# A wide column pair's sums: a tile ring of their own, made in place, at a higher priority

## The chip, the core and the metric

The kernel runs on one core of a Trainium2 chip. The metric is the device time of one execution in microseconds (us). The kernel before was timed in three runs; one further execution was recorded by the hardware profiler, and all rows come from it. Engines are named as in the profile: PE is the matrix engine (PEld its weight loads), DVE the vector engine, ACT the scalar engine, POOL the general engine, SP the engine whose queue issues the DMAs.

## The reference, cut to what matters

A batch of one sequence of 256 tokens, width 2048, goes through four layers, all in 32-bit floating point, and a last norm.

- Layer 1: norm, one input projection, sparse attention (an indexer picks 64 keys for each query) beside a multi-scale pooling branch, output projection, norm, residual; then a channel mixer: up-projection to 8192, a causal convolution over three tokens, gelu(gate) * val, down-projection.
- Layer 2: the same frame with latent attention (two low-rank projections, rotary positions) beside a gated linear recurrence, and again a channel mixer.
- Layers 3 and 4, the hybrid layers: one input projection feeds four branches of four heads each. They are attention with a forget bias (`fox`), differential attention (`diff`: the difference of two softmaxes, a norm over each head), block attention (`moba`) and gated linear attention (`gla`, with a norm over each head). Each branch's output is multiplied by silu of its gate, and an output projection adds to the residual.

The projection that the change touches is a plain matrix product, `h @ w_in` (h is 256 x 2048), whose columns are cut into these parts:

```python
h = rms_norm_2(x, norm_g)
p = split_columns(jnp.einsum("bsd,de->bse", h, w_in))
```

## The kernel before, in words

Activations are kept transposed: 128 features on the partitions, 256 tokens along the free axis. Every 32-bit factor is split into a high and a low part, and a product is high*high + low*high + high*low. Weights arrive as 899 packed tiles of 128 x 1024 (`new_sub`, L136 to L152): a DMA on SP's queue brings one in (L143), ACT copies its high part (L147), DVE subtracts to get the low part (L148). One such tile holds eight units of 128 x 128. Five raw buffers and four of each split part are kept ahead; these instructions have a priority offset of 3000.

`projT` (from L161) multiplies columns of 128 output features over all K blocks. In its wide form (n is 1 or 2 columns and there are more than four K blocks, `hold` and `hooks` unused) each column has a PSUM buffer of its own, 512 wide: the high weights meet both parts of x at once (L177, 512 columns), the low weights meet the high part of x (L178, 256 columns). So a finished column has two halves that must be added. `summed()` does it: ACT copies the second half out of PSUM (L193), DVE adds the first half to it (L194), and `evac` then works on the sum, mostly a multiplication with the norm's factor (`ev_mul`, L433). The PSUM pool `pp` has four buffers, so two wide pairs; the pool `pa`, four more, serves everything else. `projV` (from L209) makes values with the roles of the operands exchanged: over 16 K blocks 96 matmuls of 512 columns (L218 to L220), two `pp` buffers.

The order of the instructions on each engine is not written out. A planner takes the instructions in program order as priorities, works out a timeline beforehand by its own cost model, and gives each engine at each moment the ready instruction with the best priority; a tile's buffer is given out in the same process, and an instruction whose tile has no free buffer is not ready. `tc.high_priority(offset=n)` moves a block ahead by n instructions of program order (a negative n moves it back). The evacuations of projections have the offset `EVAC = 100`, the matmuls of the GLA levels -250, and the end of a layer up to 20000. On the chip each engine then executes its queue strictly in that order.

Work tiles of 128 x 2 x 256 come from the pool `wk`, tag `w2`, ten buffers, among them the two of `summed()`. Tiles of 128 x 8 x 256 come from `actp` (`a8`), 13 buffers.

In a hybrid layer (`hybrid`, from L798 on) the program order is: the first projections and `fox_q`; the GLA value projection; the six levels of GLA (DVE subtractions L936 and L937, ACT exponent L938, DVE products L940 and L941, matmuls L922, masked copies L925), its state and outputs (L956 to L994), and `norm_trans` (ACT squares L886, a square root L260, DVE scaling L891, PE transposes L896, DVE copy L897); the load of the lambda vectors (L1001, into a `w2` tile); the four pairs of `diff_q` and `diff_k` into the `a8` tile `dq`; moves of `dq` for the rotary positions; the `diff_v` projection; `fox_q`, second pair; the differential scores and values (L1036 to L1058) with `norm_trans`; `fox_k`, `fox_v`, `moba_q`, and so on.

Of the kernel before, what the change touches and what calls it, by code (L numbers as in the profile page):

```python
# [10 lines left out]
F32 = mybir.dt.float32  # L11
# [3 lines left out]
AF = mybir.ActivationFunctionType  # L15
OP = mybir.AluOpType

P = 128
T = 256
# [46 lines left out]
def kernel(  # L66
# [17 lines left out]
    ap_ = ctx.enter_context(tc.tile_pool(name="actp", bufs=13))  # L84
    rawp = ctx.enter_context(tc.tile_pool(name="rawp", bufs=5))
    hlp = ctx.enter_context(tc.tile_pool(name="hlp", bufs=4))
    wk = ctx.enter_context(tc.tile_pool(name="wk", bufs=10))
    sm = ctx.enter_context(tc.tile_pool(name="sm", bufs=6))
    pp = ctx.enter_context(tc.tile_pool(name="pp", bufs=4, space=PS))
    pa = ctx.enter_context(tc.tile_pool(name="pa", bufs=4, space=PS))  # L90
# [1 line left out]
    V, S, G, TE = nc.vector, nc.scalar, nc.gpsimd, nc.tensor  # L92

    def a8(dt=F32, shape=None):
        return ap_.tile(shape or [P, 8, T], dt, tag="a8", name="a8")

    def w2(dt=F32, shape=None):
        return wk.tile(shape or [P, 2, T], dt, tag="w2", name="w2")
# [8 lines left out]
    def pc(name, i=0, n=1):  # L107
        o, w = PRM[name]
        return prm_t[:, o + i : o + i + n]
# [42 lines left out]
    def blk(key, units=1):  # L152
        if ws["u"] == 8:
            new_sub()
        u = ws["u"]
        assert u + units <= 8
        plan.append((ws["n"] - 1, u, key))
        ws["u"] = u + units
        return ws["h"][:, u * P : (u + units) * P], ws["l"][:, u * P : (u + units) * P]

    def projT(ks, cols, key, xs, evac, hooks={}, hold=False, wide=None):  # L161


        n = len(cols)
        if wide is None:
            wide = len(ks) > 4 and n <= 2 and not hold and not hooks
        pts = [pp.tile([P, 2, T], F32, tag="pp", name="pp") for _ in range(n if wide else (n + 1) // 2)]
        for i, k in enumerate(ks):
            if i in hooks:
                hooks[i]()  # L170
            x = xs(k)
            first, last = i == 0, i == len(ks) - 1
            cs = []
            for ci, c in enumerate(cols):
                h, l = blk(key(k, c))
                if wide:
                    TE.matmul(pts[ci], h, x, start=first, stop=False, skip_group_check=True)  # L177
                    TE.matmul(pts[ci][:, 0], l, x[:, 0], start=False, stop=last, skip_group_check=True)  # L178
                    continue
                o = pts[ci // 2][:, ci % 2]  # L180
                TE.matmul(o, h, x[:, 0], start=(first and ci % 2 == 0), stop=False, skip_group_check=True)  # L181
                TE.matmul(o, l, x[:, 0], start=False, stop=False, skip_group_check=True)  # L182
                cs.append((o, h))
                if n <= 2:
                    TE.matmul(o, h, x[:, 1], start=False, stop=last, skip_group_check=True)  # L185
            if n > 2:
                for o, h in cs:
                    TE.matmul(o, h, x[:, 1], start=False, stop=last, skip_group_check=True)  # L188

        def summed():  # L190
            rest, u = w2(), w2()
            for j in range(n):
                S.activation(out=rest[:, j], in_=pts[j][:, 1], func=AF.Copy)  # L193
                V.tensor_tensor(out=u[:, j], in0=pts[j][:, 0], in1=rest[:, j], op=OP.add)  # L194
            return u

        def evacs():
            with tc.high_priority(offset=EVAC):
                if wide:
                    evac(0, summed())  # L200
                else:
                    for b in range((n + 1) // 2):
                        evac(b, pts[b])

        if hold:
            return evacs
        evacs()

    def projV(ks, key, xs, evac):  # L209
# [129 lines left out]
    class Post:  # L339
# [4 lines left out]
        def evac(self, c, ps):  # L344
            last, n = c == KT - 1, 1 if c >= KT - 2 else 2
            if c == 0:
                self.m = [a8() for _ in range(2)]
                self.acc = w2()
            with tc.high_priority(offset=20000 if last else 0):
                sq = w2() if c else self.acc  # L350
                S.activation(out=sq[:, 0:n], in_=ps[:, 0:n], func=AF.Square)
                if last:
                    self.sq = sq[:, 0]
                elif c:
                    V.tensor_tensor(out=self.acc[:, 0:n], in0=self.acc[:, 0:n], in1=sq[:, 0:n], op=OP.add)
            for j in range(n):
                V.tensor_scalar(out=self.m[(c + j) // 8][:, (c + j) % 8], in0=ps[:, j],
                                scalar1=pc(self.g, c + j), scalar2=None, op0=OP.mult)
# [994 lines left out]
```

## Time and profile before

| | us |
|---|---|
| median of the three timed runs | 2824.79 |
| lowest and highest of them | 2821.60, 2825.44 |
| profiled execution | 2810.94 |
| its span in the trace | 2809.2 |
| PE busy | 2728.4 |
| PEld busy | 2419.7 |
| DVE busy | 1919.1 |
| ACT busy | 1465.1 |

Busy time is the sum of an engine's instruction times in the span. Matmuls follow each other so closely that a matmul's own duration is longer than the distance to the next one; that distance is what counts for a row of them. PEclk is the share of its full clock that PE was granted in a stretch: 1.00 is 2.4 GHz and 0.50 is 1.2 GHz.

### The profile page before, as it was taken

How to read it: one execution, taken by the hardware profiler on the slowest of the kernel's cores; microseconds unless marked ns; L12 is line 12 of the kernel's file. 1: busy time of each engine (PE TensorE's matmuls, PEld its weight loads, DVE VectorE, ACT ScalarE, POOL GpSimd, SP SyncE). 2: the span in 40 equal slices, each digit the busy share in tenths (PEclk: the TensorE clock that was granted, in tenths of full speed). 3: DMA queues.
4: the chain of work that ended last, by engine and by line, in shares of the span. 5: the costliest groups of instructions: out<-in, count | busy, mean ns of one | idle time of the engine just before them, and what ended most of it. 6: DMA issues, size and time to landing. Idle time of an engine off the chain costs nothing.

```text
span 2809.2 us, 42670 instructions
## 1 busy us (share of the span) xinstructions
PE 2728.4 (97%) x16682; PEld 2419.7 (86%) x16682; DVE 1919.1 (68%) x3125; ACT 1465.1 (52%) x2165; POOL 5.8 (0%) x10
## 2 busy tenths in 40 slices
PE   9999999999999999999999999979899998889998
PEld 8888998888888988998888888968688997778897
DVE  6867588777655887587777655856567667465756
ACT  6455456655544675456555544634445554444554
POOL 0000000000000000000000000000000000000000
PEclk9999999999999999999999999979899998889999
DMA  7545545555555454545555555525355554434553
GB/s 252 172 166 175 190 160 188 189 192 189 189 192 167 167 184 129 188 164 185 185 186 187 188 187 180 188 85 184 114 180 169 186 181 135 139 122 160 170 186 134
DMA packets 133290, 483.45 MB, mean 172 GB/s; under 512 B 15136, under 2 KB 16224, under 8 KB 132576
## 3 DMA queue, kind: packets, MB, share of 16 engines
q1 hardware_dynamic: 133088, 480.73, 51.2%
q8 instruction: 130, 2.13, 0.3%
q14 instruction: 72, 0.59, 0.1%
HBM read 476.73 MB, written 2.10 MB: 170 GB/s over the span
## 4 chain that ended last, share of the span: by engine, by line
PE 61%; DVE 2%; ACT 1%; issue 0%; DVEq 0%; ACTq 0%
PE pp L177 25%; PE pp L178 13%; PE pp L181 4%; PE pp L182 4%; PE pp L188 2%; PE pp L218 2%; PE pp L220 2%; PE pp L219 2%; PE pp L185 1%; PE pa L424 0%; PE pa L1105 0%; PE pa L428 0%; DVE a L925 0%; PE pa L896 0%; ACT L260 0%
## 5 line engine op out<-in xcount | busy, mean ns | idle before, releaser
L177 PE MATMUL pp<-a,h 128*128 128x512 f32 x5056 | 1777.6, 396 | 3.5 <-DVE w L194 3.5
L148 DVE TENSOR_TENSOR l<-raw,h 128x1024 fp32r<-128x1024 f32 (+1 forms) x900 | 1100.6, 1223 | 735.9 <-ACT h L147 691.8
L147 ACT ACTIVATE h<-raw 128x1024 fp32r<-128x1024 f32 (+1 forms) x900 | 953.4, 1059 | 1060.6 <-PE pp L177 608.1
L178 PE MATMUL pp<-a,l 128*128 128x256 f32 x5056 | 1421.4, 281 | 0.0
L177 PEld LDWEIGHTS pp<-a,h 128*128 128x128 f32 x5056 | 949.9, 188 | 223.3 <-DVE w L194 4.1
L178 PEld LDWEIGHTS pp<-a,l 128*128 128x128 f32 x5056 | 957.7, 189 | 2.7 <-issue 1.0
L181 PE MATMUL pp<-a,h 128*128 128x256 f32 x1472 | 392.2, 288 | 15.2 <-ACT a L242 6.9
L182 PE MATMUL pp<-a,l 128*128 128x256 f32 x1472 | 389.8, 286 | 0.0
L181 PEld LDWEIGHTS pp<-a,h 128*128 128x128 f32 x1472 | 287.3, 195 | 17.3 <-ACT a L242 7.8
L182 PEld LDWEIGHTS pp<-a,l 128*128 128x128 f32 x1472 | 287.2, 195 | 0.6 <-DVE l L148 0.4
L185 PE MATMUL pp<-a,h 128*128 128x256 f32 x544 | 153.9, 283 | 0.0
L188 PE MATMUL pp<-a,h 128*128 128x256 f32 x928 | 140.6, 286 | 0.0
L218 PE MATMUL pp<-h,a 128*128 128x512 f32 x328 | 129.9, 396 | 0.0
L220 PE MATMUL pp<-h,a 128*128 128x512 f32 x328 | 129.6, 395 | 0.0
L219 PE MATMUL pp<-l,a 128*128 128x512 f32 x328 | 129.6, 395 | 0.0
L188 PEld LDWEIGHTS pp<-a,h 128*128 128x128 f32 x928 | 125.8, 196 | 0.0
L193 ACT ACTIVATE w<-pp 128x256 f32<-128x256 f32 x288 | 104.0, 385 | 12.1 <-PE pp L178 0.5
L194 DVE TENSOR_TENSOR w<-pp,w 128x256 f32<-128x256 f32 x288 | 108.4, 417 | 0.0
L577 DVE SCALAR_TENSOR_TENSOR w<-w,prm_t,w 128x255 f32<-128x255 f32 (+1 forms) x256 | 107.4, 479 | 0.2
L185 PEld LDWEIGHTS pp<-a,h 128*128 128x128 f32 x544 | 104.2, 192 | 0.0
L237 ACT ACTIVATE a<-w 128x256 fp32r<-128x256 f32 (+1 forms) x92 | 44.0, 480 | 74.8 <-DVE w L581 70.3
L220 PEld LDWEIGHTS pp<-h,a 128*128 128x128 f32 x328 | 62.6, 191 | 13.9 <-issue 1.1
(258 smaller groups left out, 1635.8 us busy)
## 6 DMA issues: line engine op xcount, KB each, us to landing
raw<-in_wpk_dram SPq DMA_DIRECT2D x898, 512.0 KB, 3.4
a<-in_cst_dram SPq DMA_DIRECT2D x2, 1024.0 KB, 5.8
x_t<-in_xT_dram SPq DMA_DIRECT2D x1, 1024.0 KB, 10.8
a<-a SPq DMA_DIRECT2D x8, 128.0 KB, 5.7
out_dram<-a SPq DMA_DIRECT2D x2, 512.0 KB, 2.7
x_t<-in_xT_dram SPq DMA_DIRECT2D x1, 640.0 KB
a<-a SPq DMA_DIRECT2D x8, 64.0 KB
out_dram<-a SPq DMA_DIRECT2D x2, 256.0 KB
```

The lines of the kernel that those rows point to most:

```text
L147: S.activation(out=h[:, a], in_=r[:, a], func=AF.Copy)
L148: V.tensor_tensor(out=l[:, a], in0=r[:, a], in1=h[:, a].bitcast(F32), op=OP.subtract)
L177: TE.matmul(pts[ci], h, x, start=first, stop=False, skip_group_check=True)
L178: TE.matmul(pts[ci][:, 0], l, x[:, 0], start=False, stop=last, skip_group_check=True)
L181: TE.matmul(o, h, x[:, 0], start=(first and ci % 2 == 0), stop=False, skip_group_check=True)
L182: TE.matmul(o, l, x[:, 0], start=False, stop=False, skip_group_check=True)
L185: TE.matmul(o, h, x[:, 1], start=False, stop=last, skip_group_check=True)
L188: TE.matmul(o, h, x[:, 1], start=False, stop=last, skip_group_check=True)
L194: V.tensor_tensor(out=u[:, j], in0=pts[j][:, 0], in1=rest[:, j], op=OP.add)
L218: TE.matmul(pts[q], xh[:, sl], h, start=(i == 0), stop=False, skip_group_check=True)
L219: TE.matmul(pts[q], xh[:, sl], l, start=False, stop=False, skip_group_check=True)
L220: TE.matmul(pts[q], xl[:, sl], h, start=False, stop=last, skip_group_check=True)
```

## The change

The pool `wk` keeps eight `w2` buffers instead of ten and gets two buffers of a second tag, `ev`, so the memory used is the same. `summed()` takes one `ev` tile instead of two `w2` tiles; the copy of the second half is written into the tile, and the sum overwrites it. The call of `summed()` moves out of the block with offset 100 into a block with offset 2500, behind only the weights' split (3000) and the ends of layers; `evac` itself stays at offset 100. Narrow projections and `projV` are as before.

```diff
-    wk = ctx.enter_context(tc.tile_pool(name="wk", bufs=10))
+    wk = ctx.enter_context(tc.tile_pool(name="wk", bufs=8))
...
         def summed():
-            rest, u = w2(), w2()
+            u = wk.tile([P, 2, T], F32, tag="ev", name="ev", bufs=2)
             for j in range(n):
-                S.activation(out=rest[:, j], in_=pts[j][:, 1], func=AF.Copy)
-                V.tensor_tensor(out=u[:, j], in0=pts[j][:, 0], in1=rest[:, j], op=OP.add)
+                S.activation(out=u[:, j], in_=pts[j][:, 1], func=AF.Copy)
+                V.tensor_tensor(out=u[:, j], in0=pts[j][:, 0], in1=u[:, j], op=OP.add)
             return u
 
         def evacs():
+            if wide:
+                with tc.high_priority(offset=2500):
+                    u = summed()
             with tc.high_priority(offset=EVAC):
                 if wide:
-                    evac(0, summed())
+                    evac(0, u)
                 else:
                     for b in range((n + 1) // 2):
                         evac(b, pts[b])
```

## Rows read from the trace of the kernel before

**Rows 1.** Page, parts 1 and 5: busy us and share; then busy, mean ns.

```profile
PE 2728.4 (97%) x16682; PEld 2419.7 (86%) x16682; DVE 1919.1 (68%) x3125; ACT 1465.1 (52%) x2165; POOL 5.8 (0%) x10
...
L148 DVE TENSOR_TENSOR l<-raw,h 128x1024 fp32r<-128x1024 f32 (+1 forms) x900 | 1100.6, 1223 | 735.9 <-ACT h L147 691.8
```

**Rows 2.** Stretches: length, then busy us of each engine, granted clock, DMA.

```profile
550.00:600.00 50.00, 50.00 (x290) 44.05 (x290) 38.30 (x58) 29.31 (x45) 0.00 (x0) 1.00 0.57 190
...
1850.00:1889.00 39.00, 23.66 (x140) 18.55 (x137) 22.46 (x60) 10.23 (x30) 0.00 (x0) 0.56 0.02 7
1970.00:1991.00 21.00, 13.68 (x44) 9.39 (x45) 12.44 (x46) 9.37 (x26) 0.00 (x0) 0.60 0.08 26
2369.00:2407.00 38.00, 22.84 (x137) 17.93 (x134) 21.58 (x60) 10.23 (x30) 0.00 (x0) 0.56 0.03 6
2486.00:2510.00 24.00, 16.43 (x59) 11.48 (x59) 14.69 (x51) 12.04 (x35) 0.00 (x0) 0.65 0.13 44
```

**Rows 3.** Waits of PE over the span: us in total, times, longest.

```profile
PE pa L896 <- DVE w L891: 24.7, 8, 3.8
...
PE pp L177 <- DVE w L194: 3.5, 2, 1.8
```

**Rows 4.** Timeline of PE, 1840 to 1890 (in brackets: idle before, its end).

```profile
1848.41 0.28 PE L178 MATMUL pp<-a,l 128*128 128x256 f32 x1
...
1853.96 1.47 PE L922 MATMUL pa<-w,w 64*128 64x128 f32 x16 [3.07 <-DVE w L941]
...
1883.81 0.80 PE L177 MATMUL pp<-a,h 128*128 128x512 f32 x1 [1.76 <-DVE w L194]
```

**Rows 5.** Timeline of ACT, 1800 to 1900 and 1900 to 2000.

```profile
1869.31 0.28 ACT L886 ACTIVATE w<-pa 128x128 f32<-128x128 f32 x1 [9.48 <-PE pa L994]
...
1879.71 0.91 ACT L193 ACTIVATE w<-pp 128x256 f32<-128x256 f32 x3
...
1982.05 0.28 ACT L886 ACTIVATE w<-pa 128x128 f32<-128x128 f32 x1 [4.84 <-PE pa L1058]
...
1984.72 1.19 ACT L193 ACTIVATE w<-pp 128x256 f32<-128x256 f32 x4
```

**Rows 6.** Timeline of DVE, 1800 to 1900.

```profile
1844.60 1.36 DVE L925 COPY_PREDICATED a<-a,pa 128x512 f32<-128x512 uint8 x2 [1.69 <-PE pa L922]
...
1860.73 1.33 DVE L925 COPY_PREDICATED a<-a,pa 128x512 f32<-128x512 uint8 x2 [0.18 <-PE pa L922]
...
1884.99 0.42 DVE L194 TENSOR_TENSOR w<-pp,w 128x256 f32<-128x256 f32 x1
1885.45 0.69 DVE L433 TENSOR_TENSOR a<-w,rb 128x512 f32<-128x512 f32 x1
```

**Rows 7.** Two stretches, columns as in Rows 2.

```profile
1849.00:1884.00 35.00, 19.66 (x140) 15.32 (x138) 20.12 (x57) 9.17 (x29) 0.00 (x0) 0.58 0.05 18
...
1955.00:1960.00 5.00, 5.00 (x30) 4.12 (x29) 4.29 (x16) 2.85 (x8) 0.00 (x0) 1.00 0.39 127
```

**Rows 8.** Timeline of PE, 1822 to 1830: projections back to back.

```profile
1821.93 0.39 PE L220 MATMUL pp<-h,a 128*128 128x512 f32 x1
1822.15 0.39 PE L177 MATMUL pp<-a,h 128*128 128x512 f32 x1
...
1822.49 0.40 PE L177 MATMUL pp<-a,h 128*128 128x512 f32 x1
```

**Rows 9.** Timeline of PE, 1940 to 1990.

```profile
1972.02 0.33 PE L896 MATMUL pa<-cst_t,w 128*128 128x128 f32 x1 [2.36 <-DVE w L891]
...
1986.30 0.80 PE L218 MATMUL pp<-h,a 128*128 128x512 f32 x1
```

**Rows 10.** Timeline of SP's queue, 1780 to 2060.

```profile
1800.23 47.78 SPq L143 DMA_DIRECT2D raw<-in_wpk_dram  x17
1869.70 0.33 SPq L1001 DMA_DIRECT2D w<-in_dlam_dram  x1
1888.90 20.93 SPq L143 DMA_DIRECT2D raw<-in_wpk_dram  x8
```


## The prediction

> **What bounds the kernel now.** I read the page first: TensorE (PE) is busy for 97% of the span, 2728.4 us of 2809.2, so only its 81 us of idle time and the places where its clock is low can be won [rows 1]. Next I read busy time and granted clock by stretches. In the steady projections PE is busy for all of 50 us at clock 1.00, and nothing done to VectorE (DVE) or ScalarE (ACT) there can save time [rows 2]. Four stretches differ, two in each hybrid layer: 39 and 21 us long in the first, 38 and 24 us in the second. In them PE is idle for 15.3, 7.3, 15.2 and 7.6 us, together 45.4 us of the 81, and the mean clock is 0.56 to 0.65, a mix of the two levels 2.4 and 1.2 GHz. The rest of the idle time lies at layer changes, which the edit leaves alone.
>
> Then the waits and the timelines say why. PE's last projection matmul before the first stretch is at 1848.41, the next at 1883.81, and that one waits 1.76 us for L194, the sum of a wide pair [rows 4]. Between them PE has only small matmuls of the gated linear attention (GLA), which arrive as DVE finishes each level. The reader is to see that the projection did not lack inputs: two pairs of `diff_q`/`diff_k` fill all four `pp` buffers, and their sums come only at 1879.71, although ACT stood idle for 9.48 us up to 1869.31, with both pairs complete since 1848.7 (1848.41 and 0.28) [rows 4, 5]. An idle engine and a finished product mean that priority is not the only thing that holds the sum; it needs two `w2` tiles, and of ten `gq`, `gk`, `cum` hold three, the GLA levels and norm scratch the others. This is an inference from the code; the trace names no tile ring. In the second stretch it is the same: ACT is idle for 4.84 us up to 1982.05, four copies of two `fox_k` pairs run from 1984.72, and the `fox_v` projection starts only at 1986.30 [rows 5, 9].
>
> **The ceiling.** A stretch loses its idle time and half of its busy time at the lower level. Time at that level is (1 - clock)/0.5 of the length: 34.3, 16.8, 33.4 and 16.8 us. If all idle time lay in it, the busy part would be 19.0, 9.5, 18.2 and 9.2 us; half of the 55.9 is 28.0, and with 45.4 this gives 73.4 us [rows 2]. But the first waits of a stretch, 3.07 and 2.36 us, come before the clock falls [rows 4, 9]; half of these, twice, adds 5.4. The ceiling is 79 us.
>
> **The change, part by part.**
>
> *Own ring, one tile for copy and sum.* It takes no instruction away: each pair keeps two copies and two sums, a sum 0.42 us [rows 6], and a sum written over its second operand is the same instruction. Bounds for in-place against separate: the trace has no such pair, so from 0 to the whole 0.42 us; I take 0, as it is off PE's path. What it moves: in the first stretch the first pair's sum goes from 1879.7 to just behind its last matmul (it begins at 1822.15 [rows 8], so near 1834 with the 11.2 us below), the second's to 1849, and PE goes on with pairs three and four. A unit of a pair (512 and 256 columns) takes 0.34 to 0.35 us [rows 8], so 32 units take 11.2 and two pairs 22.4 us. Next comes the `diff_v` projection, 96 matmuls at 0.22 us [rows 8], 21 us more, into the two `pp` buffers that pair three leaves. GLA's own matmuls, 19.66 us from 1849 to 1884 [rows 7], almost all at the low level, take some 10.5 us at the high one. So 22.4 + 10.5 = 33 us of work stand against a stretch of 35 us, and 54 us with `diff_v`.
>
> *Does `dq` have a place?* A sum tile is freed by L433, which writes `dq`. Of 13 `a8` buffers eleven are taken (four of normed x, `cA`, `cE`, `qkt`, `aux1`, `aux2`, `dsw`, `gv`); `dq` is the twelfth and `oT[1]` the thirteenth. It fits, with none to spare; `diff_v`'s output must wait for GLA's end, which holds its two `pp` buffers.
>
> *Priority 2500.* Copies and sums pass GLA's work on ACT and DVE. Per pair that is 0.84 us on each. DVE from 1849 to 1884 has 20.12 us of work, 1.1 of it sums [rows 7, 6]. Into the same time now come the splits of eight weight tiles at 1.22 [rows 1], 9.8 us, four sums, 1.7, and three L433 at 0.69 [rows 6], 2.1: 32.6 of 35 us. The GLA chain therefore ends later, by up to 13.6 us. What hides it: 54 us of PE work against 35 + 13.6 = 49. Without that cover it costs up to 13.6 us per layer. In the FFN PE is fed at DVE 38.3 of 50 us [rows 2]; the same instructions in another order there cost 0.
>
> *`w2` from ten to eight.* In the FFN a unit takes three tiles instead of five: no loss. In GLA five tiles are left beside `gq`, `gk`, `cum` instead of seven, so one level's two products and two subtractions fewer lie ready when its matmuls begin: 2 x 0.69 + 2 x 0.42 = 2.2 us per layer (by L433 and L194, whose shapes are the same) [rows 6]. Bounds: 0 (covered) to all six levels one after another (below). I take 2.2 twice, 4.4.
>
> *What stays.* PE executes in the order planned beforehand, so a transpose of `norm_trans` (L896) placed too early still stops everything behind it, next projection included. Today that is 24.7 us in eight waits [rows 3]. With projections to place in front some go; bounds 0 and 24.7, I take half, 12.4.
>
> *Second stretch.* The `fox_k` sums free `pp` at once, and `fox_v`, 21 us, fills the gap from 1969.7 (1972.02 less the wait of 2.36) to 1986.3 [rows 9]. From 1955 to 1960 scores and projections share PE, and it is busy for all 5.00 us at clock 1.00 with DVE at 4.29 [rows 7]; that is what I expect of both stretches. `fox_q` and `fox_k` come earlier too, so the softmax chain finds PE with `fox_v` and one pair of `moba_q`, 32 us, ahead of it.
>
> *Queues.* SP issues the same loads. The lambda load (L1001) waits for a `w2` tile: SP's queue issues nothing from 1848.0 to 1869.70 [rows 10]. Before, no weights are due behind it; now they are. Five raw and four split tiles, each of eight units or 2.8 us, cover 25 us, against a wait of 21.7. I take 0 and make it a rival. POOL is not touched.
>
> **The sum.** 79 - 12.4 - 4.4 = 62 us. The profiled execution took 2810.94 us (span 2809.2), so 2749 for it; the three timed runs lie 14 us higher, median 2824.79, and 62 below that is 2763.
>
> **The rivals.**
>
> *The clock stays low.* PE's idle time goes, but it still stops often enough to be granted 1.2 GHz in the four stretches: then 45.4 - 12.4 = 33 us are won, 2792. For it: in each of these stretches the clock is mostly at the lower level while PE is busy over half of the time [rows 2]. Against: where projections run between the small matmuls, 1955 to 1960, it is 1.00 [rows 7]. The Trainium skill, "TensorE: Matmul & The Clock Gate", section "A second HAM failure mode: psum-queue depth-cycling", speaks against the change: PE that cycles through PSUM banks can stop briefly between groups so often that its clock swings; by that rule the time would be this 2792. The steady row at 1.00, which cycles through the same four buffers, does not agree with it.
>
> *Two tiles are too few.* If `dq`'s evacuation is not run while GLA fills DVE, pair three's sum waits, `diff_v` cannot start, and PE stops after 33 us until a chain that ends 13.6 + 2.2 us later: 22.4 - 15.8 = 7 us per layer, some 2811 for both with nothing in the second stretch.
>
> *The change does nothing.* If something else than `w2` held the sums (a thirteenth buffer, or the plan's own times), the order stays: 2825.
>
> *Slower.* Place: GLA's levels. One level alone is 2.2 on DVE, matmuls of 1.47 [rows 4] and masked copies of 1.36, 5.0 us; today six levels start from 1844.60 to 1860.73, 3.2 apart [rows 6]. With five tiles they may follow one another: 1.8 x 6 = 11 us per layer, 22 for both, 2847. It decides if PE has no projection meanwhile, that is if SP's wait for L1001 outlasts the 25 us of staged weights. For it: 21.7 us of wait is close. Against: the loads are planned before it when due.
>
> **How the numbers follow.** Forecast 0.58 (its own range 2746, the ceiling, to 2780), low clock 0.14, two tiles 0.09, nothing 0.07, slower 0.12. The measurement can tell about 0.2%, 5.6 us. Faster 0.81, within 0.2% 0.07, slower 0.12. The range 2740 to 2808 holds the first two and most of the third.
>
> **What would show it.** Right: L193 behind each pair's last matmul near 1834 and 1849; L177 without a gap in 1849 to 1870; clock 1.00 there; L218 of `fox_v` before the last L1056. Wrong: L177's gap still there; or L177 running at 1.2 GHz; or PE waiting for L148 behind L1001. A longer GLA chain (last L897 past 1890) with PE busy is expected and does no harm.

## The result, and the profile after

The changed kernel takes 2753.23 us (median of 4 runs, 2752.46 to 2756.35) where the kernel before took 2824.94 (4 runs beside it, 2821.6 to 2825.44): a ratio of 0.9751, 95% interval 0.9734 to 0.9768, 71.7 us less. The forecast was 2763.

| | before | after |
|---|---|---|
| profiled execution (span), us | 2810.94 (2809.2) | 2752.46 (2750.7) |
| PE busy, idle in the span, us | 2728.4, 80.8 | 2710.5, 40.2 |
| mean granted clock | 0.977 | 0.994 |
| first mixer, first FFN, us | 353.7, 541.7 | 353.4, 550.6 |
| second mixer, second FFN, us | 298.7, 550.0 | 298.0, 550.9 |
| first, second hybrid layer, us | 563.3, 485.1 | 529.8, 451.3 |

The layers run from one closing column sum to the next (the start of its first matmul, L282 before, L285 after: lines from 196 on are 3 higher in the changed kernel). All of the gain lies in the two hybrid layers, 33.5 and 33.8 us. The first FFN of the profiled execution of before is 8.9 us shorter than after, and at least 8 us shorter than in every other profile here, so the two traces differ by 58.5 us and not by 67; the last section comes back to it. From here on, a time after is some 9 us later than its counterpart before.

The page of the changed kernel, parts 1 and 5, answers [rows 1]: instructions are the same in number, PE is idle for 40.6 us less, and the sum written over its second operand takes 416 ns, as before.

```profile
PE 2710.5 (99%) x16682; PEld 2397.9 (87%) x16682; DVE 1915.6 (70%) x3125; ACT 1460.9 (53%) x2165; POOL 5.8 (0%) x10
...
L194 DVE TENSOR_TENSOR ev<-pp,ev 128x256 f32<-128x256 f32 x288 | 108.2, 416 | 0.7 <-ACT ev L193 0.5
```

Stretches of the changed kernel, columns as in [rows 2]: the four places that were starved. The clock is 1.00 in all four and PE is busy for 47.7 to 50.0 of 50 us. The last two lines are details of the first, and the reader is to look at DVE there: 5.00 and 4.77 of 5 us. While the later GLA levels run, from 1855 to 1880, DVE is nearly full (23.7 of 25 us), as the sum of its work had said; over the whole 50 us of the first line it is not (39.39). Of these two lines only the last shows PE short of work.

```profile
1850.00:1900.00 50.00, 47.73 (x340) 38.37 (x339) 39.39 (x79) 20.55 (x41) 0.00 (x0) 1.00 0.37 120
1950.00:2000.00 50.00, 49.45 (x261) 39.51 (x260) 36.40 (x95) 31.23 (x67) 0.00 (x0) 1.00 0.48 158
2350.00:2400.00 50.00, 48.11 (x301) 39.12 (x298) 35.70 (x71) 22.09 (x42) 0.00 (x0) 1.00 0.40 133
2450.00:2500.00 50.00, 49.96 (x262) 39.45 (x261) 31.63 (x84) 26.02 (x55) 0.00 (x0) 1.00 0.43 137
...
1855.00:1860.00 5.00, 5.00 (x35) 3.94 (x33) 5.00 (x10) 2.08 (x4) 0.00 (x0) 1.00 0.35 112
...
1895.00:1900.00 5.00, 3.74 (x19) 3.01 (x19) 4.77 (x11) 1.77 (x4) 0.00 (x0) 1.00 0.41 133
```

ACT's timeline of the changed kernel answers [rows 5]. Copies of the first two pairs come at 1842.81 and 1857.90, each right behind its pair's last matmul; before, they stood behind the GLA's end. The third and the fourth come together at 1894.52, though, after a stretch without any.

```profile
1842.81 0.73 ACT L193 ACTIVATE ev<-pp 128x256 f32<-128x256 f32 x2
...
1857.90 0.73 ACT L193 ACTIVATE ev<-pp 128x256 f32<-128x256 f32 x2 [2.01 <-PE pp L178]
...
1894.52 1.18 ACT L193 ACTIVATE ev<-pp 128x256 f32<-128x256 f32 x4
```

DVE's timeline of the changed kernel answers [rows 6] and says why. L928 (L925 before) closes a GLA level: the six begin from 1854.12 to 1875.58, 4.3 us apart, where they were 3.2 apart. L436 (L433 before), which frees a sum tile, first comes at 1892.83, right behind the first L900 (L897 before), although the first sum was made from 1843.87 on. The last L900 is at 1900.23; before, its counterpart was at 1882.08. So the GLA ends some 9 us later against the shifted clock.

```profile
1854.12 1.35 DVE L928 COPY_PREDICATED a<-a,pa 128x512 f32<-128x512 uint8 x2 [1.69 <-PE pa L925]
...
1875.58 1.35 DVE L928 COPY_PREDICATED a<-a,pa 128x512 f32<-128x512 uint8 x2
...
1892.16 0.75 DVE L900 TENSOR_SCALAR a<-pa,prm_t 128x512 f32<-128x512 f32 x1 [1.70 <-PE pa L899]
1892.83 0.68 DVE L436 TENSOR_TENSOR a<-ev,rb 128x512 f32<-128x512 f32 x1
...
1893.59 0.66 DVE L436 TENSOR_TENSOR a<-ev,rb 128x512 f32<-128x512 f32 x1
...
1895.82 1.41 DVE L194 TENSOR_TENSOR ev<-pp,ev 128x256 f32<-128x256 f32 x4
...
1900.23 0.75 DVE L900 TENSOR_SCALAR a<-pa,prm_t 128x512 f32<-128x512 f32 x1
```

PE's timeline of the changed kernel answers [rows 4, 9]. The transposes L899 (L896 before) follow without idle time; `diff_v` (L221, L218 before) starts at 1896.29 and waits for a sum, but for 1.26 us only; `fox_v` starts at 1957.62, where it had started at 1986.30, and runs among the softmax's matmuls.

```profile
1888.70 0.30 PE L899 MATMUL pa<-cst_t,w 128*128 128x128 f32 x1
...
1896.29 0.50 PE L221 MATMUL pp<-h,a 128*128 128x512 f32 x1 [1.26 <-DVE ev L194]
...
1957.62 0.39 PE L221 MATMUL pp<-h,a 128*128 128x512 f32 x1
```

The waits of PE in the changed kernel answer [rows 3]. The 24.7 us of L896 for L891 are gone altogether (as L899 for L894 they would stand first); in their place are 2.5 us for the third pair's sum, once in each hybrid layer. The first three waits, at layer changes and at the start of the kernel, are as before. The last line shown is one of the two waits of the GLA's matmuls for its products: 12.4 us together before (6.3 and 6.1), 1.5 us now (0.8 and 0.7).

```profile
PE pn L299 <- DVE dg L298: 7.5, 5, 1.7
PE pp L181 <- ACT a L245: 6.9, 4, 1.7
PE pp L181 <- ACT h L147: 5.3, 1, 5.3
PE pp L221 <- DVE ev L194: 2.5, 2, 1.3
...
PE pa L925 <- DVE w L944: 0.8, 2, 0.4
```

SP's queue in the changed kernel answers [rows 10]: weights are issued up to 1896.26 (1819.73 and 76.53), through the whole of the GLA, and the lambda load (L1004, L1001 before) comes behind them, at 1896.31.

```profile
1819.73 76.53 SPq L143 DMA_DIRECT2D raw<-in_wpk_dram  x22
1896.31 0.46 SPq L1004 DMA_DIRECT2D w<-in_dlam_dram  x1
```

### The profile page after: what moved, and what is told of

It reads as the page before. It is cut to its first block, busy times and chain, and to the rows that moved or that the text cites. A ratio compares the mean times of both kernels' runs of the same rounds, so it can differ in the third digit from the quotient of the medians.

```text
span 2750.7 us, 42666 instructions
## 1 busy us (share of the span) xinstructions
PE 2710.5 (99%) x16682; PEld 2397.9 (87%) x16682; DVE 1915.6 (70%) x3125; ACT 1460.9 (53%) x2165; POOL 5.8 (0%) x10
## 4 chain that ended last, share of the span: by engine, by line
PE 61%; DVE 2%; ACT 0%; issue 0%; DVEq 0%; ACTq 0%
PE pp L177 25%; PE pp L178 13%; PE pp L181 4%; PE pp L182 4%; PE pp L188 2%; PE pp L221 2%; PE pp L223 2%; PE pp L222 2%; PE pp L185 1%; PE pa L427 0%; PE pa L1108 0%; PE pa L431 0%; DVE l L148 0%; PE pa L925 0%; PE pa L1111 0%; PE pa L739 0%
## 5 line engine op out<-in xcount | busy, mean ns | idle before, releaser
L178 PE MATMUL pp<-a,l 128*128 128x256 f32 x5056 | 1423.3, 282 | 0.0
L178 PEld LDWEIGHTS pp<-a,l 128*128 128x128 f32 x5056 | 955.4, 189 | 4.0 <-issue 1.7
L221 PE MATMUL pp<-h,a 128*128 128x512 f32 x328 | 128.8, 393 | 2.5 <-DVE ev L194 2.5
L193 ACT ACTIVATE ev<-pp 128x256 f32<-128x256 f32 x288 | 104.6, 383 | 23.9 <-PE pp L178 11.5
L194 DVE TENSOR_TENSOR ev<-pp,ev 128x256 f32<-128x256 f32 x288 | 108.2, 416 | 0.7 <-ACT ev L193 0.5
L221 PEld LDWEIGHTS pp<-h,a 128*128 128x128 f32 x328 | 61.7, 188 | 16.3 <-DVE ev L194 3.2
```

The source lines that it names most:

```text
L194: V.tensor_tensor(out=u[:, j], in0=pts[j][:, 0], in1=u[:, j], op=OP.add)
L221: TE.matmul(pts[q], xh[:, sl], h, start=(i == 0), stop=False, skip_group_check=True)
```

## The experiments

Theory A: the sums were held for want of `w2` tiles, and the ring of their own is the gain. Theory B: the priority of 2500 is. Each part was run alone first.

**The ring alone.** The changed kernel with the sums at the old priority.

```diff
-                with tc.high_priority(offset=2500):
+                with tc.high_priority(offset=EVAC):
                     u = summed()
```

> The ring of its own and the sum in place, but copy and sum stay at offset 100. Theory A (a sum waits because the ten w2 buffers are held by gated linear attention and softmax work, so a ring of its own is what frees the four PSUM buffers): nearly the whole gain, 2753 to 2765 us; in the first hybrid layer L193 runs right behind each diff pair, PE has no gap over 2 us there and the clock stays at 1.00. Theory B (the sum waits because work of better priority stands ahead of it on ACT and DVE): about 2825 us, the four starved stretches as before.

Measured: 2754.55 us (2753.07 to 2756.29), ratio 0.9752 [0.9738, 0.9767] to the kernel before: the whole gain. Its first stretch (columns as in [rows 2]) is full:

```profile
1840.00:1910.00 70.00, 68.04 (x440) 55.42 (x439) 50.89 (x94) 29.62 (x53) 0.00 (x0) 1.00 0.43 145
```

Its ACT timeline has the copies 0.3 us later than the changed kernel:

```profile
1843.12 0.73 ACT L193 ACTIVATE ev<-pp 128x256 f32<-128x256 f32 x2
...
1858.21 0.73 ACT L193 ACTIVATE ev<-pp 128x256 f32<-128x256 f32 x2 [2.01 <-PE pp L178]
```

Theory A holds; with the ring there, the priority is worth nothing that can be measured. It only moves a wait: here PE waits 2.6 us for L894 at L899, in the changed kernel 2.5 us for L194 at L221. A shared ring of more than ten buffers was not run; the run with the halved need, below, is the nearest to it.

**The priority alone.** The kernel before, two `w2` of ten for each pair as there.

```diff
         def evacs():
+            if wide:
+                with tc.high_priority(offset=2500):
+                    u = summed()
             with tc.high_priority(offset=EVAC):
                 if wide:
-                    evac(0, summed())
+                    evac(0, u)
```

> Offset 2500 for copy and sum, but two w2 tiles out of ten as before, not in place. Theory A: the sums are first in line for a buffer but still have to wait until two are free, and they take them from the attention levels; part of the gain, 2765 to 2805 us. Theory B: the whole gain, 2753 us. If neither, 2825 us.

Measured: 2825.48 us (10 runs, 2823.43 to 2827.36), ratio 1.0004 [0.9995, 1.0013]. This was a miss even for theory A, which had left the priority some of the gain. In this stretch of it PE has 54.66 of 70 us at clock 0.76:

```profile
1840.00:1910.00 70.00, 54.66 (x337) 44.88 (x336) 39.91 (x82) 21.37 (x43) 0.00 (x0) 0.76 0.24 83
```

On ACT the picture is that of [rows 5]: 9.50 us idle with two complete pairs (the last L178 before it starts at 1860.94), and the four copies only after the squares of the GLA's second norm.

```profile
1881.84 0.28 ACT L889 ACTIVATE w<-pa 128x128 f32<-128x128 f32 x1 [9.50 <-PE pa L997]
...
1892.23 1.18 ACT L193 ACTIVATE w<-pp 128x256 f32<-128x256 f32 x4
```

And the wait of PE is back to the last digit:

```profile
PE pa L899 <- DVE w L894: 24.7, 8, 3.8
```

The sums stand 2500 places ahead and come as late as before: here priority did not obtain a buffer.

**In place alone.** The kernel before with one `w2` a pair instead of two.

```diff
-            rest, u = w2(), w2()
+            u = w2()
             for j in range(n):
-                S.activation(out=rest[:, j], in_=pts[j][:, 1], func=AF.Copy)
-                V.tensor_tensor(out=u[:, j], in0=pts[j][:, 0], in1=rest[:, j], op=OP.add)
+                S.activation(out=u[:, j], in_=pts[j][:, 1], func=AF.Copy)
+                V.tensor_tensor(out=u[:, j], in0=pts[j][:, 0], in1=u[:, j], op=OP.add)
```

> One w2 tile instead of two for a pair, ten buffers, offset 100. Theory A: one free buffer is enough, but the levels of better priority take it first: 2795 to 2825 us, sums in the starved stretches still tens of us late. Theory B: 2825 us. The sum's own duration stays 0.42 us in either.

Measured: 2824.25 us (10 runs, 2821.8 to 2827.38), ratio 1.0000 [0.9991, 1.001]. Half the need from the shared ring is no help; the sum keeps its 0.42 us.

**One tile in the ring.** The changed kernel with one `ev` tile instead of two.

```diff
-            u = wk.tile([P, 2, T], F32, tag="ev", name="ev", bufs=2)
+            u = wk.tile([P, 2, T], F32, tag="ev", name="ev", bufs=1)
```

> As the changed kernel, with one ev tile instead of two. In the changed kernel dq was written only at 1892.8 us, so both ev tiles were held from 1844 on. Theory A with that: with one tile the second pair's sum waits too, PE can run one pair (11.2 us) less per hybrid layer before it stops, and the clock falls in what is left: 22 to 40 us slower than the changed kernel, 2775 to 2793 us. Rival (a held tile is no limit, the planner runs L436 early when it is needed): 2753 us.

Measured: 2774.61 us (2773.57 to 2777.2), ratio 0.9824 [0.981, 0.9839], 20.1 us above the kernel with the ring alone that ran beside it (2774.61 less 2754.55), just under the low end of what was expected. The first stretch has lost part of its work again:

```profile
1840.00:1910.00 70.00, 63.08 (x393) 51.89 (x392) 45.61 (x88) 26.30 (x49) 0.00 (x0) 0.85 0.34 114
```

Its ACT timeline shows the second pair's copy waiting for L436, that is, for the one tile to come free:

```profile
1844.11 0.73 ACT L193 ACTIVATE ev<-pp 128x256 f32<-128x256 f32 x2
...
1893.31 0.66 ACT L193 ACTIVATE ev<-pp 128x256 f32<-128x256 f32 x2 [3.98 <-DVE a L436]
```

The second stretch stays full (from 1950 to 2010 PE is busy for 59.55 us at clock 1.00), so one tile does for `fox_k` and two are needed for `diff_q` and `diff_k`. In the profile the two hybrid layers are 11.9 and 11.0 us longer than in the changed kernel (541.7 and 462.3 us), near one pair of matmuls (11.2 us) each. DVE's timeline shows when `dq` is first written:

```profile
1891.92 0.75 DVE L900 TENSOR_SCALAR a<-pa,prm_t 128x512 f32<-128x512 f32 x1 [0.91 <-PE pa L899]
1892.59 0.68 DVE L436 TENSOR_TENSOR a<-ev,rb 128x512 f32<-128x512 f32 x1
```

The last group of the GLA's output matmuls L997, which read `aux1` and `aux2`, starts only at 1894.44 here, so L436 does not wait for it.

**Why does L436 come so late?** Theory T: it has no buffer for `dq`. Its rival, theory S: it is passed over on DVE, since its priority stayed at 100. Three kernels were run beside the changed kernel itself, and two more after them. What was expected of the changed kernel, run again:

> The changed kernel itself, run beside the next three as their yardstick: 2753 us in any theory, with L436 (dq) first at about 1893 us.

Measured: 2751.56 us (2749.8 to 2753.41), ratio 0.9748 [0.9735, 0.9762].

**The priority for L436 too.**

```diff
             if wide:
                 with tc.high_priority(offset=2500):
-                    u = summed()
-            with tc.high_priority(offset=EVAC):
-                if wide:
-                    evac(0, u)
-                else:
+                    evac(0, summed())
+            else:
+                with tc.high_priority(offset=EVAC):
```

> As the changed kernel, but what follows a wide pair's sum (ev_mul and the like) also gets offset 2500. In the changed kernel dq is written only at 1892.8 us although its sums are there from 1844 on. Theory S (that is a matter of priority: GLA's work stands ahead of L436): L436 runs right behind the first sum, near 1845 us, the waits of L221 for L194 (2.5 us in two) go, 2746 to 2751 us. Theory T (dq has no a8 buffer until norm_trans has written its output): L436 stays near 1893 us, 2752 to 2755 us.

Measured: 2753.28 us (2750.81 to 2755.39), ratio 0.9754 [0.9741, 0.9767]. On its DVE timeline (lines here 2 lower than in the changed kernel) L434 still comes right behind the first L898:

```profile
1895.81 0.75 DVE L898 TENSOR_SCALAR a<-pa,prm_t 128x512 f32<-128x512 f32 x1 [1.70 <-PE pa L897]
1896.48 1.29 DVE L434 TENSOR_TENSOR a<-ev,rb 128x512 f32<-128x512 f32 x2
```

A higher priority does not bring it forward.

**A third tile in the ring.** Seven `w2`, three `ev`.

```diff
-    wk = ctx.enter_context(tc.tile_pool(name="wk", bufs=8))
+    wk = ctx.enter_context(tc.tile_pool(name="wk", bufs=7))
...
-            u = wk.tile([P, 2, T], F32, tag="ev", name="ev", bufs=2)
+            u = wk.tile([P, 2, T], F32, tag="ev", name="ev", bufs=3)
```

> Three ev and seven w2 tiles, memory the same. If the two ev tiles are what stops PE for 1.26 us before L221 in each hybrid layer, this wait goes and the third pair is summed near 1875 us: 2749 to 2752 us. If the w2 tiles are now short for the GLA levels (four left beside gq, gk and cum), the chain ends later and PE waits for it: 2755 to 2765 us.

Measured: 2749.09 us (2747.52 to 2750.16), ratio 0.9739 [0.9726, 0.9752]. The third pair is copied at 1873.23 and PE's 2.5 us of waiting are gone, while L436 comes no earlier than 1896.94.

**A fourth, with six `w2`.**

```diff
-    wk = ctx.enter_context(tc.tile_pool(name="wk", bufs=8))
+    wk = ctx.enter_context(tc.tile_pool(name="wk", bufs=6))
...
-            u = wk.tile([P, 2, T], F32, tag="ev", name="ev", bufs=2)
+            u = wk.tile([P, 2, T], F32, tag="ev", name="ev", bufs=4)
```

> Four ev and six w2 tiles: prices the narrower w2 ring by taking it further. GLA has three tiles left beside gq, gk and cum, so its six levels run one after another, 1.8 us or more longer each, 11 us per layer. If PE's work covers that: 2749 to 2756 us, with all four diff pairs summed before GLA ends. If not: 2760 to 2785 us, with PE waiting for L944 or L894 and the clock falling.

Measured: 2753.13 us (5 runs, 2750.02 to 2756.14), ratio 0.9757 [0.9743, 0.977]. Two `w2` fewer and two `ev` more than in the changed kernel come out even in the runs. The run changes both at once, so a cost of the one and a gain of the other could cancel.

**`dq` claimed before the GLA.** A `memset` on GpSimd, which the changed kernel does not have, takes the buffer ahead of the GLA's own.

```diff
         gv = value("gla_v")
+        dq = a8()
+        G.memset(dq, 0.0)
...
-        dq = a8()
         for i, nm in enumerate(("diff_q", "diff_k")):
```

> As the changed kernel, but dq is taken and cleared by POOL before GLA, so that it has its a8 buffer when the first sum is there. If it was the buffer that kept L436 at 1892 us (even offset 2500 left it right behind the first write of norm_trans's output): L436 runs near 1844 and 1859, pairs three and four are summed at once, PE no longer waits 1.26 us before L221, 2747 to 2751 us. If it was not: L436 stays near 1892, 2751 to 2755 us.

Measured: 2748.52 us (5 runs, 2744.8 to 2750.27), ratio 0.9738 [0.9725, 0.9751]. On its DVE timeline L436 follows each sum, the first three long before the first L900:

```profile
1840.32 0.75 DVE L194 TENSOR_TENSOR ev<-pp,ev 128x256 f32<-128x256 f32 x2
1841.17 0.69 DVE L436 TENSOR_TENSOR a<-ev,rb 128x512 f32<-128x512 f32 x1
...
1856.74 0.69 DVE L436 TENSOR_TENSOR a<-ev,rb 128x512 f32<-128x512 f32 x1
...
1876.44 0.68 DVE L436 TENSOR_TENSOR a<-ev,rb 128x512 f32<-128x512 f32 x1
...
1887.91 0.75 DVE L900 TENSOR_SCALAR a<-pa,prm_t 128x512 f32<-128x512 f32 x1 [1.43 <-PE pa L899]
...
1893.15 0.68 DVE L436 TENSOR_TENSOR a<-ev,rb 128x512 f32<-128x512 f32 x1
```

`diff_v` starts at 1891.17 without a wait, and the stretch is the fullest of those with two tiles:

```profile
1840.00:1910.00 70.00, 69.24 (x445) 56.98 (x444) 51.29 (x95) 30.98 (x51) 0.00 (x0) 1.00 0.43 145
```

So theory T is right: with the buffer given out early, L436 comes early at its old priority. It is a buffer again, this time that of `dq`.

**Both.** `dq` claimed early (the edit above), with three `ev` and seven `w2`:

```diff
-    wk = ctx.enter_context(tc.tile_pool(name="wk", bufs=8))
+    wk = ctx.enter_context(tc.tile_pool(name="wk", bufs=7))
...
-            u = wk.tile([P, 2, T], F32, tag="ev", name="ev", bufs=2)
+            u = wk.tile([P, 2, T], F32, tag="ev", name="ev", bufs=3)
```

> The two that could help together: dq taken early, three ev and seven w2 tiles. If both remove the same wait, no better than either alone: 2747 to 2751 us. If the third ev tile helps elsewhere too (fox_k and moba_k pairs): 2744 to 2748 us.

Measured: 2749.79 us (2749.14 to 2750.26), ratio 0.9741 [0.9727, 0.9754]: no better than either alone. Both mend the same 2.5 us of waiting. That `dq` early and the third tile lie some 3 us below the changed kernel (2748.52, timed beside another series of the kernel before, and 2749.09, against 2751.56) fits that size, but the intervals of the ratios overlap, so the runs do not tell them apart from it. The profiles, one execution each, point the same way: the two hybrid layers together take 981.1 and 980.1 us in the two profiles of the changed kernel and 980.3 with the priority for L436, against 977.7 with three tiles, 977.6 with four, 975.9 with `dq` early and 977.0 with both.

## Why the prediction was right, and where its steps were not

**What bounds the kernel: right.** The inference that had no row of its own, that two shared `w2` tiles held the sums, is shown by the ring alone (2754.55 us) against the priority alone (2825.48) and the halved need alone (2824.25). For the first two pairs the order of events was right to the microsecond: copies expected near 1834 and 1849 are, with the shift of 8.8 us, at 1842.81 and 1857.90.

**The ceiling: right in kind.** Of the 79 us 67.3 were won in the two hybrid layers. PE's idle time fell by 40.6, of 45.4 that were counted there. The other 26.7 is busy time, 17.9 by the pages plus the 8.8 by which the untouched layers, the first FFN above all, were quicker in the profile of before; 28.0 and 5.4 were counted for it.

**The deductions: too large, and this is the miss.** The step "What stays" sized the waits of L896 at 12.4 us, half of 24.7 for want of anything better; the wait is 0 now. With projections to put in front, each transpose finds its scaled rows ready. And "`w2` from ten to eight" took 4.4 us for later GLA levels: they did come later, 4.3 us apart instead of 3.2, but PE had work beside them, and even six tiles, with four `ev`, did not lengthen the run. Neither deduction came as described.

**The sum of PE's work: too small.** What was lost of the ceiling, 11.5 us (67.3 against 78.8 before rounding), lies elsewhere. Of idle time 4.8 us stay in the four places: 2.5 us for the third pair's sums, 2.0 us for the GLA's levels and state. Of busy time 6.7 us less were won than counted. Here the term "22.4 + 10.5 = 33 us of work" is at fault: from 1857.70, where pair three begins, to 1896.28 PE is busy for 36.3 us at clock 1.00, although four of the eight transposes come later, and the same holds from 2342.52 to 2381.10 in the second hybrid layer. That is 3.4 us more in each, in sum near the 6.7. The sum added the two kinds of matmuls as if each ran by itself. In the timeline the mix is dearer at its seams: a projection matmul just behind GLA matmuls has its successor 0.34 us later (1857.24 to 1857.58), the next one 0.23 us later (1857.70 to 1857.93). No run separates this loss further. So it is in part luck that the sum came within 10 us: losses that it did not have took the place of deductions that did not come.

**`dq`: wrong.** It was counted as the twelfth of thirteen buffers, free throughout the GLA. It was not written before 1892.83, so both `ev` tiles stayed taken, pairs three and four stayed in `pp`, and `diff_v` was no cover for the GLA at all: of the 54 us only the first term was there, 33 us by the sum and 36.3 by the trace. This is the state that the rival "two tiles are too few" describes. Its stop was priced at 15.8 us per layer and cost 1.26. PE's own work, with short waits in it, lasted to 1895.02 (1894.74 and 0.28), 37.3 us behind the second pair instead of 33. And `dq` had its buffer 35 us behind the second pair, right after the first L900, where the price had let it wait for the end of a chain of 35 + 15.8 us. One tile fewer shows the price where the cover is really gone: 20.1 us. What gave `dq` its buffer is left open. The run with one tile speaks against the last matmuls L997, since L436 runs before they start there (1892.59 against 1894.44); in every kernel here that does not claim `dq` early it runs behind the first L900. Why the plan gave none sooner, although thirteen were there by count, no run shows.

**The other rivals.** The clock does not stay low: 1.00 in all four stretches. The Trainium skill, "TensorE: Matmul & The Clock Gate", section "A second HAM failure mode: psum-queue depth-cycling", tells of a kernel that cycles through PSUM banks and whose PE stops between groups of matmuls so often that its clock swings. This kernel cycles through the same four `pp` buffers as before, PE is busy for 47.7 us or more of 50 in the four places, and the clock did not swing; a kernel that stops as often as that one was not run. The slower case fell at its condition: the lambda load is issued behind the weights that the GLA's stretch needs, and PE has no wait for weights behind it. The GLA's longer chain was as forecast and harmless.

**From the trace to the runs.** Taking 62 us from the median gave 2763; the runs came out 9.8 us below. In the profiles of the kernels with the priority alone and in place alone, whose hybrid layers work as before, these take 1051.0 and 1050.1 us, against 1048.4 in the profile of before and 981.1 after: 69 to 70 us, near the 71.7 of the medians. The rest, 2 us, is within the runs' spread. So of the 9.8 us some 5 are the deductions (16.8 us against 11.5 lost), 2 to 3 the quicker hybrid layers in the profile of before, and the rest is not settled.

The Trainium skill, "Perfetto Trace Analysis", section "Optimization Strategy", says that a gap that repeats on the engine which should be full can mean that the next tile found no room in SBUF or PSUM. The trace agrees for PSUM: PE's next pair waits for the sum that frees its buffers [rows 4]. That the sum in turn lacked an SBUF tile no row names; the runs show it, since the ring for that tile alone is worth 69.0 us (2823.58 less 2754.55).

## What to carry to other kernels

Where a product is complete, the engine that should move it is idle, and it is not moved, look for the buffer that the move writes to; give what frees PSUM a ring that no long-lived tile can hold, and try that before priorities, which got no buffer in either run here. Follow the chain one link on: the next holder (here `dq`) becomes the new limit, and whether it costs anything depends on how much work the bound engine still has in front of it. A wait that exists only because an engine's order has nothing else to put there should be counted as gone when work arrives, not halved: PE's 24.7 us for L891 became 0 here, and 7.5 us where one tile let the work run short. And where two kinds of matmuls are to share PE, look for a stretch in which they already do, instead of adding their times.

## What the runs showed of the hardware

In these traces the granted clock does not tell all of PE's pace. In the profile of before, the first FFN's main matmul took 391 ns each, all alike, 1155 of them in 400 us:

```profile
L177 PE MATMUL pp<-a,h x1155: 391/391/391, 449.6 to 849.7; 128*128 128x512 f32 x193
```

In the profile of the changed kernel the same stretch has 1134 of 395 to 403 ns, and in every other profile here, and from 1300 to 1700 in that of before, there are 1133 or 1134 of 394 to 404 ns:

```profile
L177 PE MATMUL pp<-a,h x1134: 395/398/403, 449.6 to 850.0; 128*128 128x512 f32 x189
```

The clock is 1.00 in both. A pace 1.8% higher (21 of 1155) over most of that layer's 542 us makes the 8.9 us in the table, which are the larger part of the 14 us by which the profiled execution of before lay under its median. Its cause is open. Whoever subtracts one trace from another should first compare layers that the edit doesn't touch.
